# Hybrid attention encoder block on one core: order of the gate products, slots of the attention tile, loads and first bank of the merge

## Chip, core and metric

The kernel runs on one core of one Trainium2 chip, as one launch. The metric is the device time of one execution in microseconds; the three runs of the kernel before took 1425.70, 1423.99 and 1425.23 us, and the median is 1425.23 us. The execution that was profiled took 1424.24 us.

The engines are named as in the profile: PE is TensorE's matrix product and PEld its weight load, DVE is VectorE, ACT is ScalarE, POOL is GpSimd, and SP is the queue that issues almost all DMAs. SBUF is the memory that the engines compute from, PSUM the eight banks into which PE writes.

## What is computed

One encoder block on 1024 tokens of width 1024, with 16 meta tokens put in front. The part that matters here, cut from the reference:

```python
proj = h @ w_in                       # h: normed tokens; the last 2 x 1024 columns are the gates ga, gb
y_a = differential_attention(qa, ka, va, ...)     # 4 heads, two softmax maps each, 8 tiles of 128 queries
y_b = windowed_gqa(qb, kb, vb, sink)              # 8 heads, a window of 3 blocks and the meta tokens
merged = jax.nn.sigmoid(ga) * (y_a @ w_ba) + jax.nn.sigmoid(gb) * (y_b @ w_bb)
h = h + merged @ w_out
h = h + swiglu(rms_norm(h, norm_ffn), w_gate, w_up, w_down)
```

In a tile of the differential attention the first map's exponentials are combined with the second map's, each with its own sum of the row (`attn = softmax(s1) - lam * softmax(s2)`), and the combined map is multiplied with the values; the output is normed by the mean of its squares.

## The kernel before

All big products are made in a single-pass float32 form, with operands split in a high and a low half: a product of two operands is three matmuls (high x high, high x low, low x high). The parts of the program in order of time: the norm and the projections, with the windowed attention between them; the differential attention, into whose gaps the products of the gates are filled; the merge of the two branches with the gates; the output product; the feed-forward part.

**The gates.** The 2048 gate columns are eight pairs k of 128 + 128 columns (`G_COLS`). The tokens are cut in two halves, the width in two halves too, so each pair is a 2x2 block product, made with seven products p = 1 to 7 instead of eight (Strassen's scheme in Winograd's form). (k,p) is product p of pair k. It is four steps of three matmuls of 128x512, and a step is what `fill(1)` emits: one `next` of the generator `gate_steps` (line 827). `order_g` (lines 732 to 735) is the order of the 56 products. In a first phase (24 products, `first_g`) each pair has products 1, 6 and 2, then in a second phase products 5, 7, 3 and 4 of every pair. The order of pairs 0 to 3 in the first phase is made of two pairs at a time: product 1 of both, product 2 of both, so that the bank that holds (k,1) rests for a product before (k,2) adds into it. Between the two, ACT copies the bank, because the value of (k,1) alone is needed as well (line 887). Pair 4 has its products 1 and 2 one right after the other, pairs 5, 6 and 7 with product 6 among them or behind them.

**Weights of the gates.** `weights_g` (line 761) makes the operand of product n on POOL, up to three products ahead of PE (`ensure_g(n + 4)`, line 920): sums where the scheme needs them (two for product 6, lines 777 and 778), the cast to the high half (line 799) and the low half (line 800). The raw weights are loaded by `load_g` (line 747) in 512 KB pieces into four buffers, in the order in which they are used, a piece when the piece four places before it is done with. A pair k < 5 loads its first half for products 1 and 2, and both halves again for product 6 later on; a pair k >= 5 loads both halves for 1, 6 and 2.

**What is kept.** Product 6 adds to the value of product 1. For a pair k < 5 that value is stored to `u_d[k]` in HBM and read back (`k_next`, line 857) some products before its product 6; for the others it stays in SBUF (line 891). After product 6 the sum is stored to `u_d[k]` again, and read once more in the second phase, where ACT copies it into a PSUM bank (line 864) as the start of product 5.

**Token sums.** Products 6, 5, 7 and 4 need sums of token blocks, which were made earlier and lie in HBM (`t_d`). `turn_into(i)` (line 811) loads one of them (2 MB) over a block of the normed tokens `hT`: sum 2 before the first product 6 (issued behind the load `raws_g[5]`, line 818), sum 0 after (7,6), sums 1 and 3 after the last product 6 (`LAST_T`, line 808).

**Banks.** Gate products use two PSUM banks of the pool `psum2` in turn, with tags pp0 and pp1. `take` (line 849) gives a product the bank that is free and was used longest ago.

**The attention tile.** Tile n (0 to 31, four heads of eight) runs through the slots of `SLOTS` (line 41): "s" emits a piece of its scores (`scores_a`, three pieces for the second map, then three for the first; DVE reduces them at lines 980 and 984, ACT takes the exponential at 988), "t" a turn (transposition) of the tile before (`transpose_a`, ACT copies the high half at 1009, DVE subtracts the low half at 1010), "g" a gate step, and "n" a piece of the values or of the norm of tiles before that (`values_a`, line 1013, three parts for two tiles; `normed_a`, line 1023, which has a sum of squares and a factor on PE and waits between them). At the end of a tile's slots stands its combination on DVE (line 994), and the next tile's turns read its result. At the start of head 0, `G_FIRST` = 24 steps go first, at the start of the other heads `G_HEAD` = 6. Of the 224 steps `HOLD` = 22 are held back from the tiles (line 1050): they are filled in behind the last tile, one after each value part and norm piece, then the rest together.

PE's and, up to line 1100, POOL's instructions run in the order in which the program is written; the other engines' orders are chosen by the scheduler of the language, which estimates a timeline.

**Towards the merge.** As soon as the last value part frees the attention's memory (line 1127), SP loads two pieces of `w_bb` and the windowed attention's output yb (eight pieces of 256 KB, line 1142), ACT and DVE split yb (`split_yb`, line 1152; the second pair of tiles needs the memory that the gate weights leave, line 1168). The merge (line 1268) makes 32 products of 12 matmuls (`gated`, line 1256), with a sigmoid gate each. They take banks from two tags of four of the pool `psum3` in turn, "bank" (`ps_bank`) and "bank_t" (`ps_bank_t`). `psum3` takes over the banks of `psum2`; a tag gets its banks when it is first asked for.

Of the kernel before, what the change touches and what calls it, by code (L numbers as in the profile page):

```python
# [39 lines left out]
COMBINE_POOL = (0, 1, 2, 3)  # L40
SLOTS = "ssgsgntssgsgntgnt"
SLOTS_LAST = "ggggntgntnt"
S_BUFS = (2, 2)
AT_BUFS = 2
G_BUFS = 3
ROOM = 16
HOLD = 22
GT_BUFS = 4
# [26 lines left out]
def encoder_block(ctx: ExitStack, tc: tile.TileContext, x, meta, norm_mix, w_in, lq1, lk1, lq2, lk2,  # L75
                  subln, sink, w_ba, w_bb, w_o, norm_ffn, w_g, w_u, w_d, norm_final, out, dbg=None):
    nc = tc.nc
# [653 lines left out]
    G_COLS = [C_GB + 2 * k * P for k in range(4)] + [C_GA + 2 * k * P for k in range(4)]  # L731
    first_g = [(k, p) for i in (0, 2) for p in (1, 2) for k in (i, i + 1)] + [(4, 1), (4, 2)]
    first_g += [kp for k in (5, 6) for kp in ((k, 1), (k, 6), (k, 2), (k - 5, 6))]
    first_g += [(7, 1), (7, 2), (7, 6), (2, 6), (3, 6), (4, 6)]
    order_g = first_g + [(k, p) for k in range(8) for p in (5, 7, 3, 4)]
    n_first = len(first_g)

    uses_g = []
    for n, (k, p) in enumerate(order_g):
        if n >= n_first:  # L740
            uses_g.append([("s", k, 1), ("s", k, 0)] if p == 5 else [])
        else:
            uses_g.append({1: [("f", k, 0)], 2: [], 6: [("f", k, 1)] if k >= 5 else [("m", k, 0), ("m", k, 1)]}[p])
    loads_g = [u for us in uses_g for u in us]
# [16 lines left out]
    def weights_g(n):  # L761
# [3 lines left out]
        nm = f"{k}_{p}"  # L765
        kind = "s" if n >= n_first else "m" if p == 6 and k < 5 else "f"
        wa, wb = raw_g[kind, k, 0], raw_g.get((kind, k, 1))
# [3 lines left out]
        if p == 1:  # L771
            src = a11
        elif p == 2:
            src = a12
            n_freed[0] += 1 if k < 5 else 2 if k < 7 else 0
        elif p == 6:
            tt(a21, a21, a22, ALU.add)
            tt(a21, a21, a11, ALU.subtract)
            src = a21
            if k < 5 or k == 7:  # L780
                n_freed[0] += 2
        elif p == 5:
            src = sums_g[k] = gwork.tile([P, 4, P], F32, tag="s", name=f"s1g_{k}", bufs=1)
            tt(src, a21, a22, ALU.add)
        elif p == 7:
            tt(a21, a11, a21, ALU.subtract)
            src = a21
        elif p == 3:
            tt(a12, a12, a11, ALU.add)
            tt(a12, a12, sums_g.pop(k), ALU.subtract)  # L790
            src = a12
        else:
            src = a22
            n_freed[0] += 2
# [12 lines left out]
    RIGHT_G = {1: (0, 0), 6: (0, 1), 2: (1, 0), 5: (0, 0), 7: (0, 1), 3: (1, 1), 4: (1, 0)}  # L807
    LAST_T = {(7, 6): (0,), (4, 6): (1, 3)}
    INTO_T = {2: (0, 1), 0: (0, 0), 1: (0, 1), 3: (1, 0)}

    def turn_into(i):

        d, t = INTO_T[i]
        for c in (range(4) if i == 1 else (slice(0, 4),)):
            for hl, h in enumerate((hT_hi, hT_lo)):
                with ExitStack() as after:
                    if i == 2:
                        after.enter_context(tc.issue_after(raws_g[5].ins))
                    elif i == 0:
                        after.enter_context(tc.issue_after(values_in[1].ins))  # L820
                    elif i == 3:
                        after.enter_context(tc.issue_after(turned_t[0].ins))
                    to = f32(h)[:, 4 * d:4 * d + 4, HALF[t]]
                    last = nc.sync.dma_start(to[:, c], t_d[i][:, hl, c])
        turned_t[i] = last

    def gate_steps():
# [27 lines left out]
        for n, (k, p) in enumerate(order_g):  # L855
            ensure_g(n + 1)
            k_next = {(5, 1): 0, (6, 1): 1, (7, 1): 2, (7, 6): 3, (2, 6): 4, (3, 6): 0}.get((k, p), k + 1 if p == 7 and k < 7 else None)
            if k_next is not None:
# [20 lines left out]
            for c in range(4):  # L879
# [4 lines left out]
                if c == 3:  # L884
                    if p == 1:
                        p1 = kept_g(f"p1_{k}")
                        nc.scalar.copy(p1, ps)
                        if k < 5:
                            held_stores.append((u_d[k], p1))
# [194 lines left out]
    for n in range(AH * NT + T_LAG):  # L1084
# [36 lines left out]
        if n >= T_LAG and tiles[n - T_LAG][1] % 2:  # L1121
            tail.append(later(tiles[n - T_LAG]))
    n_gates[0] += HOLD
    while not valued:
        step_tail()
        fill(1)
    close_apool()
# [10 lines left out]
    for o, raw in enumerate((a11[:, 2], asum[:, 0])):  # L1138
        nc.sync.dma_start(raw.rearrange("p (c n) -> p c n", n=P), w_bb[:, o * P:(o + 1) * P].rearrange("(c p) n -> p c n", p=P))
    for j in range(4):  # L1140
        for h in range(2):
            nc.sync.dma_start((a12, w11)[h][:, j], yb_d[j // 2][j % 2 * P:j % 2 * P + P, h * 512:h * 512 + 512])
# [8 lines left out]

    def split_yb(p, j0):
        for j in (j0, j0 + 1):
            yb_t.append(p.tile([P, 2, S], F32R, name=f"yb{j}"))
        for h in range(2):
            cols = slice(h * 512, h * 512 + 512)
            for k in (j0, j0 + 1):
                split(yb_t[k][:, 0, cols], yb_t[k][:, 1, cols], (a12, w11)[h][:, k], nc.vector)

    ybpool, close_yb = pool("ybpool")  # L1160
    split_yb(ybpool, 0)
    while tail:
# [5 lines left out]
    ybpool2, close_yb2 = pool("ybpool2")  # L1168
    split_yb(ybpool2, 2)
    order_pe.__exit__(None, None, None)  # L1170
# [85 lines left out]
    def gated(i, o, half, w, src):  # L1256
# [4 lines left out]
        n_gated[0] += 1  # L1261
        ps = (ps_bank if n_gated[0] % 2 else ps_bank_t)(f"ppa_{o}_{half}_{i}")
        branch_mm(ps, w, src, tk)
# [607 lines left out]
```

## Time and profile before

| | |
|---|---|
| median of three runs | 1425.23 us |
| the profiled execution | 1424.24 us, its span 1421.9 us |
| PE busy in the span | 1401.0 us (99%) |
| DVE, ACT, POOL busy | 914.8, 672.1, 636.7 us |
| moved by DMA | 228.27 MB |
| granted TensorE clock, mean of the span | 0.998 |

All times below are in microseconds from the start of the profiled span. A row of a timeline is: start, duration, engine, line, operation, what it writes <- what it reads, sizes, count, and in brackets the idle time of the engine before it and what ended that. Matmuls overlap: a matmul of 128x512 lasts 0.39 and the next starts 0.23 after it, so a short idle time of PE in the profile is somewhat less than what was lost. A row of a list of waits is: who waited <- for whom: us in total, number, longest.

### The profile page before, as it was taken

The page shows a single profiled execution, that of the slowest core. Times are in us where ns is not written, and L with a number is a line of the kernel's source. Part 1 is how long each engine was busy: PE and PEld are TensorE (multiplying, and loading weights), DVE is VectorE, ACT ScalarE, POOL GpSimd, SP SyncE. Part 2 cuts the span into 40 slices and gives each one's busy share as a digit, 9 for nine tenths or more (in the row PEclk, how much of TensorE's full clock was granted, in tenths as well). Part 3 has the DMA queues.
Part 4 walks back from the last instruction along what each step waited for, and adds up shares of the span by engine and source line. Part 5 has one row for each costly group of instructions (what it writes and reads, how often), then busy time and mean ns, then how long its engine had stood idle before and what let it go on. Part 6 is the DMA issues. An engine that isn't in the chain of part 4 may idle for free.

```text
span 1421.9 us, 20667 instructions
## 1 busy us (share of the span) xinstructions
PE 1401.0 (99%) x7183; PEld 1202.7 (85%) x7183; DVE 914.8 (64%) x1584; ACT 672.1 (47%) x1284; POOL 636.7 (45%) x648
## 2 busy tenths in 40 slices
PE   9999999998999999999999999999999999999998
PEld 8998999987888888878888888888888888888886
DVE  6555666527787878666978956544555453787566
ACT  6355556435445555455346644333333333444454
POOL 4156865546677666322503055555545441000442
PEclk9999999999999999999999999999999999999999
DMA  8446565386896363296522724433333323954343
GB/s 235 92 128 184 154 199 160 106 290 225 259 318 211 105 209 105 68 342 198 149 103 90 207 90 148 148 106 98 101 111 104 97 97 110 353 186 144 120 128 144
DMA packets 194297, 228.27 MB, mean 161 GB/s; under 512 B 16824, under 2 KB 127360, under 8 KB 194192
## 3 DMA queue, kind: packets, MB, share of 16 engines
q1 hardware_dynamic: 192272, 224.11, 49.3%
q10 hardware_dynamic: 1920, 2.83, 0.7%
q8 instruction: 57, 0.93, 0.3%
q14 instruction: 48, 0.39, 0.1%
HBM read 152.48 MB, written 67.86 MB: 155 GB/s over the span
## 4 chain that ended last, share of the span: by engine, by line
PE 90%; DVE 4%; DMA 2%; ACT 1%; issue 1%; SPq 1%; POOL 1%; ACTq 0%; POOLq 0%; DVEq 0%
PE pg L1634 29%; PE pd L1738 14%; PE pg L881 8%; PE ppa L721 6%; PE po L1537 4%; PE pp_va L230 3%; PE pp_ka L230 3%; PE aps L977 3%; PE pp_qa L230 3%; PE apy L1019 3%; PE pp_qb L230 3%; PE bps L397 2%; PE po L1545 2%; PE bpy L437 1%; PE apt L1006 1%; PE bpt L432 1%
## 5 line engine op out<-in xcount | busy, mean ns | idle before, releaser
L1634 PE MATMUL pg<-t,wop 128*128 128x512 f32 x1056 | 242.5, 389 | 0.0
L1634 PEld LDWEIGHTS pg<-t,wop 128*128 128x128 f32 x1056 | 198.3, 188 | 41.1
L120 POOL TENSOR_TENSOR wop<-wf,wop 128x512 fp32r<-128x512 f32 x114 | 153.9, 1351 | 162.4 <-ACT wop L119 148.7
L1738 PE MATMUL pd<-ob,oa 128*128 128x512 f32 x924 | 210.1, 390 | 0.2 <-DVE ob L120 0.2
L1738 PEld LDWEIGHTS pd<-ob,oa 128*128 128x128 f32 x924 | 173.4, 188 | 36.8 <-DVE ob L120 1.0
L1634 PE MATMUL pg<-b,wop 128*128 128x512 f32 x792 | 183.3, 390 | 0.0
L1634 PEld LDWEIGHTS pg<-b,wop 128*128 128x128 f32 x792 | 148.5, 188 | 30.7
L881 PE MATMUL pg<-hT_hi,wopg 128*128 128x512 f32 x448 | 169.9, 400 | 2.7 <-POOL wopg L800 1.8
L119 ACT ACTIVATE wop<-wf 128x512 fp32r<-128x512 f32 x128 | 80.8, 633 | 73.4 <-PE pg L1634 44.3
L120 POOL TENSOR_TENSOR oa<-ra,oa 128x512 fp32r<-128x512 f32 x27 | 34.9, 1294 | 169.4 <-ACT oa L119 167.7
L119 ACT ACTIVATE oa<-ra 128x512 fp32r<-128x512 f32 x77 | 48.7, 632 | 109.0 <-PE pd L1738 50.8
L988 ACT ACTIVATE as<-as,amn 128x1040 f32<-128x1040 f32 x64 | 74.5, 1165 | 50.6 <-DVE amn L984 50.4
L881 PEld LDWEIGHTS pg<-hT_hi,wopg 128*128 128x128 f32 x448 | 84.3, 188 | 15.5 <-POOL wopg L800 2.2
L1411 DVE TENSOR_TENSOR s<-wf,wf 128x512 f32<-128x512 f32 x22 | 17.6, 798 | 112.2 <-DMA wf<-in_w_ff_up_dram 70.7
L977 PE MATMUL aps<-ak,aq 128*128 128x352 f32 (+1 forms) x384 | 86.6, 334 | 2.4 <-DVE amn L980 2.2
L881 PE MATMUL pg<-hT_lo,wopg 128*128 128x512 f32 x224 | 88.2, 394 | 0.0
L980 DVE CUSTOM_DVE_ANT_0 as<-aps,dist,far_a 128x704 f32<-128x704 f32 x64 | 60.3, 943 | 34.9 <-PE aps L977 34.6
L399 DVE CUSTOM_DVE_ANT_0 bs<-bps,tbx,nsink 128x432 f32<-128x432 f32 (+1 forms) x64 | 38.6, 629 | 61.6 <-PE bps L397 37.8
L1009 ACT ACTIVATE at<-apt 128x512 fp32r<-128x512 f32 (+1 forms) x96 | 45.4, 484 | 63.0 <-PE apt L1006 63.0
L977 PEld LDWEIGHTS aps<-ak,aq 128*128 128x128 f32 x384 | 64.2, 189 | 12.2 <-DVE amn L980 4.7
L409 POOL TENSOR_SCALAR bs<-bs,bdn 128x432 f32<-128x432 f32 (+1 forms) x64 | 36.9, 596 | 75.3 <-DVE bdn L407 34.4
L1019 PEld LDWEIGHTS apy<-at,av 128*128 128x128 f32 x400 | 54.2, 190 | 4.0
(321 smaller groups left out, 3131.1 us busy)
## 6 DMA issues: line engine op xcount, KB each, us to landing
ra<-aop SPq DMA_DIRECT2D x77, 256.0 KB, 2.7
wf<-in_w_ff_gate_dram SPq DMA_DIRECT2D x25, 512.0 KB, 3.8
wf<-in_w_ff_up_dram SPq DMA_DIRECT2D x25, 512.0 KB, 3.8
aop<-as SPq DMA_DIRECT2D x44, 256.0 KB, 2.1
w_c<-in_w_in_dram SPq DMA_DIRECT2D x17, 512.0 KB, 4.8
aop<-c SPq DMA_DIRECT2D x33, 256.0 KB, 2.0
ak<-ka_d SPq DMA_DIRECT2D x16, 520.0 KB, 6.5
t_d<-tst SPq DMA_DIRECT2D x16, 512.0 KB, 3.8
```

The lines of the kernel that those rows point to most:

```text
L119: high = nc.scalar.activation(hi, src, AF.Copy)
L120: lo_eng.tensor_tensor(lo, src, f32(hi), ALU.subtract)
L230: product = nc.tensor.matmul(ps[:, :n], a[:, c, :], b[:, c, at:at + n], start=(u == 0), stop=(u == 3 * DC - 1))
L721: nc.tensor.matmul(ps, w[:, a, j, :], src(j, b, tk), start=(j == 0 and n == 0), stop=(j == 3 and n == 2))
L881: nc.tensor.matmul(ps, op[:, x, c, :], h[:, 4 * d + c, HALF[t]], start=(p in (1, 6, 7) and c == 0 and i == 0), stop=(p in (2, 6, 3, 4) and ...
L977: nc.tensor.matmul(ps[:, :n], qs[m][:, t * P:(t + 1) * P], ks[m][:, vv, k0:k0 + n], start=(vv == 0), stop=(vv == 1))
L980: nc.vector.tensor_tensor_reduce(s[m][:, 0:2 * n].rearrange("p (a k) -> p a k", a=2), two[:, :, :n], dist[:, u0:u0 + 2 * n].rearrange("p ( ...
L988: nc.scalar.activation(s[m][:, 0:L], s[m][:, 0:L], AF.Exp, bias=mn[:, m, 1:2], scale=-1.0, accum_out=dn[:, 1:2] if m else first_sum)
L1019: nc.tensor.matmul(py[:, cols], v[:kp, a, k, :], at_[:kp, k, b, :], start=(k == 0 and j == 0), stop=(k == 8))
L1537: nc.tensor.matmul(sets_o[p][u], oa[:, a, u * P:(u + 1) * P], ob[:, b, :], start=(p in (1, 5) and j == 0 and k == 0), stop=(p in (2, 3) an ...
L1634: nc.tensor.matmul(ps, op[:, x, c, :], b[:, y, c, :], start=(p in (1, 5) and c == 0 and n == 0), stop=(p in (4, 2, 3) and c == 3 and n == ...
L1738: nc.tensor.matmul(ps[u], oa[:, a, u * P:(u + 1) * P], ob[:, b, :], start=(p in (1, 2, 5) and j == 0 and k == 0), stop=(p in (2, 3, 4) and ...
```

## The change

Six things change; no arithmetic of the result does.

- `order_g`: pairs 4 and 5 join the pattern of two pairs at a time. Then follow (6,1), (6,6), (6,2), (0,6), (7,1), (7,2), (7,6) and (1,6) to (5,6). Pair 5 now belongs to those whose product 1 goes through HBM and whose weights are loaded again for product 6, and the reads of the kept sums are put to other products.
- Token sum 2 is issued behind the load `raws_g[6]`; sums 1 and 3 follow (5,6), which is the last product 6 now.
- `SLOTS`: a gate step moves from behind the sixth score piece to ahead of the first turn. `SLOTS_LAST` has places for four gate steps, all at its front, instead of four there and a fifth behind the first turn.
- `HOLD` is 16. Behind the last tile two steps are filled in, and none between the value parts.
- yb is loaded and split by halves of the tokens: all four tiles' first half, then the second.
- `gated` begins with the other tag of banks.

```diff
-SLOTS = "ssgsgntssgsgntgnt"
-SLOTS_LAST = "ggggntgntnt"
+SLOTS = "ssgsggntssgsntgnt"
+SLOTS_LAST = "ggggntntnt"
...
-HOLD = 22
+HOLD = 16
...
-    first_g = [(k, p) for i in (0, 2) for p in (1, 2) for k in (i, i + 1)] + [(4, 1), (4, 2)]
-    first_g += [kp for k in (5, 6) for kp in ((k, 1), (k, 6), (k, 2), (k - 5, 6))]
-    first_g += [(7, 1), (7, 2), (7, 6), (2, 6), (3, 6), (4, 6)]
+    first_g = [(k, p) for i in (0, 2, 4) for p in (1, 2) for k in (i, i + 1)]
+    first_g += [(6, 1), (6, 6), (6, 2), (0, 6), (7, 1), (7, 2), (7, 6)] + [(k, 6) for k in range(1, 6)]
...
-            uses_g.append({1: [("f", k, 0)], 2: [], 6: [("f", k, 1)] if k >= 5 else [("m", k, 0), ("m", k, 1)]}[p])
+            uses_g.append({1: [("f", k, 0)], 2: [], 6: [("f", k, 1)] if k >= 6 else [("m", k, 0), ("m", k, 1)]}[p])
...
-            n_freed[0] += 1 if k < 5 else 2 if k < 7 else 0
+            n_freed[0] += 1 if k < 6 else 2 if k < 7 else 0
...
-    LAST_T = {(7, 6): (0,), (4, 6): (1, 3)}
+    LAST_T = {(7, 6): (0,), (5, 6): (1, 3)}
...
-                        after.enter_context(tc.issue_after(raws_g[5].ins))
+                        after.enter_context(tc.issue_after(raws_g[6].ins))
...
-            k_next = {(5, 1): 0, (6, 1): 1, (7, 1): 2, (7, 6): 3, (2, 6): 4, (3, 6): 0}.get((k, p), k + 1 if p == 7 and k < 7 else None)
+            k_next = {(6, 1): 0, (7, 1): 1, (7, 6): 2, (1, 6): 3, (2, 6): 4, (3, 6): 5, (4, 6): 0}.get((k, p), k + 1 if p == 7 and k < 7 else None)
...
-                        if k < 5:
+                        if k < 6:
                             held_stores.append((u_d[k], p1))
...
     n_gates[0] += HOLD
+    fill(2)
     while not valued:
         step_tail()
-        fill(1)
...
-    for j in range(4):
-        for h in range(2):
+    for h in range(2):
+        for j in range(4):
             nc.sync.dma_start((a12, w11)[h][:, j], yb_d[j // 2][j % 2 * P:j % 2 * P + P, h * 512:h * 512 + 512])
...
-    def split_yb(p, j0):
+    def open_yb(p, j0):
         for j in (j0, j0 + 1):
             yb_t.append(p.tile([P, 2, S], F32R, name=f"yb{j}"))
-        for h in range(2):
-            cols = slice(h * 512, h * 512 + 512)
-            for k in (j0, j0 + 1):
-                split(yb_t[k][:, 0, cols], yb_t[k][:, 1, cols], (a12, w11)[h][:, k], nc.vector)
+
+    def split_yb(j0, h):
+        cols = slice(h * 512, h * 512 + 512)
+        for k in (j0, j0 + 1):
+            split(yb_t[k][:, 0, cols], yb_t[k][:, 1, cols], (a12, w11)[h][:, k], nc.vector)
 
     ybpool, close_yb = pool("ybpool")
-    split_yb(ybpool, 0)
+    open_yb(ybpool, 0)
+    split_yb(0, 0)
...
-    split_yb(ybpool2, 2)
+    open_yb(ybpool2, 2)
+    for j0, h in ((2, 0), (0, 1), (2, 1)):
+        split_yb(j0, h)
...
-        ps = (ps_bank if n_gated[0] % 2 else ps_bank_t)(f"ppa_{o}_{half}_{i}")
+        ps = (ps_bank_t if n_gated[0] % 2 else ps_bank)(f"ppa_{o}_{half}_{i}")
```

More of the change, by code (lines that the diff above doesn't have):

```diff
@@ L765, in weights_g @@
         nm = f"{k}_{p}"
-        kind = "s" if n >= n_first else "m" if p == 6 and k < 5 else "f"
+        kind = "s" if n >= n_first else "m" if p == 6 and k < 6 else "f"
         wa, wb = raw_g[kind, k, 0], raw_g.get((kind, k, 1))
@@ L779, in weights_g @@
             src = a21
-            if k < 5 or k == 7:
+            if k < 6 or k == 7:
                 n_freed[0] += 2
```

## The prediction

> **What bounds the kernel now.** I read the page first, then the busy time by stretches of 50 us, then the list of waits of the whole execution, and last the timelines around each wait.
>
> ```profile
> span 1421.9 us, 20667 instructions
> PE 1401.0 (99%) x7183; PEld 1202.7 (85%) x7183; DVE 914.8 (64%) x1584; ACT 672.1 (47%) x1284; POOL 636.7 (45%) x648
> ...
> 290.00:615.00 325.00, 314.21 (x1868) 277.69 (x1866) 228.69 (x508) 160.38 (x296) 199.91 (x232) 1.00 0.61 204
> ...
> 400.00:450.00 50.00, 48.77 (x299) 43.29 (x298) 41.58 (x93) 25.87 (x48) 39.69 (x44) 1.00 0.84 295
> ...
> 600.00:650.00 50.00, 49.15 (x222) 40.12 (x221) 29.74 (x42) 28.18 (x48) 14.80 (x12) 1.00 0.94 312
> 650.00:700.00 50.00, 50.00 (x222) 41.26 (x221) 42.27 (x53) 20.15 (x35) 20.34 (x14) 1.00 0.51 157
> ```
>
> The columns after the stretch are its length and the busy us of PE, weight load, DVE, ACT and POOL. TensorE is the bound: 1401.0 of 1421.9 us. The whole change lies between 290 and 615 us (differential attention with the gate products filled in) and in the merge behind it. There TensorE idles 325.00 - 314.21 = 10.8 us, and behind it nothing is left to win: 650 to 700 us is full. The change adds and removes no matrix product, so 10.8 us bounds the gain, and the question is which waits end. Here they are:
>
> ```profile
> PE apt L1006 <- DVE at L1010: 2.3, 4, 0.8
> PE aps L977 <- DVE amn L980: 2.2, 7, 0.4
> PE pg L881 <- POOL wopg L800: 1.8, 1, 1.8
> PE apt L1006 <- DVE as L994: 1.7, 1, 1.7
> ...
> PE apt L1006 <- DVE adn L991: 1.0, 1, 1.0
> ...
> PE pg L881 <- ACT p L887: 0.8, 1, 0.8
> PE ppa L721 <- DVE g L912: 0.8, 1, 0.8
> ...
> PEld aps L977 <- DVE amn L980: 4.7, 10, 0.6
> ```
>
> Total, number and longest stand behind each pair; the last row is of the stretch 290 to 660. The seven PE rows add to 10.6 us. Each one that stands once is one place, and four of those five are places that the change rewrites.
>
> **The change, part by part.** I write (k,p) for product p of gate pair k, a step for a quarter of it (three matmuls), and count steps in the program's order to find the tile in which each falls.
>
> The price of a step, and the four places:
>
> ```profile
> 376.18 4.12 PE pg L881 x18
> ...
> 324.61 0.53 PE L881 MATMUL pg<-hT_hi,wopg 128*128 128x512 f32 x1 [0.85 <-ACT p L887]
> ...
> 338.89 0.51 PE L881 MATMUL pg<-hT_hi,wopg 128*128 128x512 f32 x1 [1.76 <-POOL wopg L800]
> ...
> 592.29 0.66 PE L1006 MATMUL apt<-ident,as 128*128 128x128 f32 x4 [1.72 <-DVE as L994]
> ...
> 615.11 7.11 PE L721 MATMUL ppa<-yb,wbhb 128*128 128x512 f32 x30 [0.78 <-DVE g L912]
> ```
>
> Eighteen matmuls are six steps, so one step is 4.12/6 = 0.69 us.
>
> *a. Pairs 4 and 5 in one another's gaps.* At 324.61 (4,2) waits 0.85 us, because it adds into the bank of (4,1), which ACT must copy first. After, (5,1) stands between them in the other bank. But its weights are barely there:
>
> ```profile
> 322.74 1.29 POOL L800 TENSOR_TENSOR wopg<-wg_f,wopg 128x512 fp32r<-128x512 f32 x1
> ...
> 328.82 1.29 POOL L777 TENSOR_TENSOR wg_f<-wg_f 128x512 f32<-128x512 f32 x1 [4.80 <-DMA wg_f<-in_w_in_dram]
> ...
> 313.87 0.36 SPq L824 DMA_DIRECT2D hT_hi<-t_d  x1
> 316.56 0.36 SPq L824 DMA_DIRECT2D hT_lo<-t_d  x1
> ...
> 319.33 0.39 SPq L757 DMA_DIRECT2D wg_f<-in_w_in_dram  x1
> ```
>
> The low half of (5,1), tenth or eleventh on POOL, ended at 322.74 + 1.29 = 324.03, when TensorE was free at 323.76. A gain between 0 (POOL keeps that order and is late) and 0.85; I take 0.55, as two thirds of the wait is nearer to these rows than none.
>
> *b. The product that waited for a load.* At 338.89 TensorE waits 1.76 us for the weights of (5,6), whose load was issued at 319.33 behind the 2 MB of the token sum (the two hT rows) and landed 9.5 us later, at 328.82. After, this place computes (5,2) from a load that POOL already had at 322.74, (6,6) comes two products later, and the token sum (two DMAs of 1 MB) is issued behind one more weight load. It is not needed before (6,6) either, so it has as much time as before. So the wait goes. Does it come back at the next stop? The chain behind a tile's turn starts from TensorE's own scores and shifts along with them, so I take 1.76, with 0.8 as the low end (the wait of 1.0 on L991, two turns later, grows to twice its length).
>
> *c. A new wait.* (7,1) and (7,2) are products 16 and 17 now. Steps 66 to 71 are the six filled in one go at the head of attention head 1: the last two of (7,1), then all of (7,2), in one bank. In place of (7,1) stands (6,2) now, and its copy shows the price:
>
> ```profile
> 377.17 0.63 PE L881 MATMUL pg<-hT_hi,wopg 128*128 128x512 f32 x2
> ...
> 377.61 0.59 ACT L894 COPY g<-pg 128x512 f32<-128x512 f32 x1 [1.11 <-PE pg L881]
> ```
>
> The first matmul of the row at 377.17 ends (6,2) at 377.56, the second begins the next product some 0.24 after it, at 377.41. ACT is free (1.11 us idle), starts 0.05 after the end and is done at 378.20, so TensorE would go on at about 378.25: a loss of 0.8, for all that is queued behind on it, the next tile's scores first. Low end 0.6; high end 2.0, if an exponential of 1.17 us goes ahead on ACT (the row in d).
>
> *d. The moved gate steps.* A tile keeps six score pieces, five gate steps and three turns; one gate step goes from behind the sixth score piece to ahead of the first turn. Between a tile's last scores and the turn that needs its combination there are four gate steps before and after, so the cover of that chain does not grow. What changes is that the second turn comes one step (0.69 us) sooner, so its eviction (L1010) can be over before the combination (L994) starts:
>
> ```profile
> 365.24 1.16 ACT L988 ACTIVATE as<-as,amn 128x1040 f32<-128x1040 f32 x1
> ...
> 325.06 1.28 DVE L994 SCALAR_TENSOR_TENSOR as<-as,adn,as 128x1040 f32<-128x1040 f32 x1
> ...
> 366.85 2.25 DVE L994 SCALAR_TENSOR_TENSOR as<-as,adn,as 128x1040 f32<-128x1040 f32 x1
> 369.02 0.87 DVE L1010 TENSOR_TENSOR at<-apt,at 128x512 fp32r<-128x512 f32 x2
> 369.82 0.93 DVE L980 CUSTOM_DVE_ANT_0 as<-aps,dist,far_a 128x704 f32<-128x704 f32 x1
> ...
> 366.70 1.30 POOL L800 TENSOR_TENSOR wopg<-wg_m,wopg 128x512 fp32r<-128x512 f32 x1
> ```
>
> Now the order on DVE is combination, two evictions (0.87), then the reduction that the next scores wait for. Taking the evictions out of that row could give up to 3.0, two thirds of the 4.5 us that the waits on L1010 and on L980 hold. Other way: if the second turn's copy on ACT now goes ahead of the exponential, the chain is longer by some 0.5 us where the scores are already waiting, ten places by the PEld row: a loss of 5. I take a gain of 0.5, near nothing, because the chain and its cover stay.
> A rule speaks against even that. The combination took 2.25 us beside a POOL weight step (366.70) and 1.28 alone. The Trainium skill (SBUF — State Buffer, Who interferes with whom) says that a VectorE instruction with two SBUF inputs contends with a GpSimd instruction that reads SBUF; the trace agrees, with 0.97 us in this row. By it the eviction order would not matter in the tiles that meet a POOL step, and the sum would be 3.2, without this 0.5.
>
> *e. The last tile.* At 592.29 the last combination is waited for, 1.72 us, because the gate budget is spent. After (16 steps held back instead of 22, shorter last slots) one gate step and four more stand in that place.
>
> ```profile
> 586.97 0.47 PE L977 MATMUL aps<-ak,aq 128*128 128x336 f32 x2
> ...
> 597.88 0.99 PE L1019 MATMUL apy<-at,av 128*128 128x256 f32 x7
> ```
>
> The chain took from the last scores to the turn 592.29 - 586.97 = 5.3 us. The cover will be five steps (3.45) and two value parts (0.99 and more each), 5.4, with the factor's and the second turn's transpositions on top. The wait goes: 1.72, between 1.0 and 2.1 (with 0.4 of a wait on L980 one turn earlier).
>
> *f. The merge.* Of the steps behind the last value part (ended 598.87) 14 stay of 20. Now that stretch lasts to 615.11 - 0.78 = 614.33, 15.5 us: 20 steps of 0.69 and 1.7 of other work. After: 14 x 0.69 + 1.7 = 11.3. Its first product waits 0.78 for L912, the eviction of (7,4). As each pool's banks lie in the order in which they are first asked for, asking the other tag first gives the first product the same bank again, but the new product order puts (7,3) there, which ACT copies. What that copy stands behind:
>
> ```profile
> 611.40 1.68 ACT L119 ACTIVATE yb<-m 128x512 fp32r<-128x512 f32 x3 [2.31 <-DMA m<-yb_d]
> 613.09 1.28 ACT L1260 ACT_TABLE_LOAD   x1
> 614.38 0.63 ACT L1260 ACTIVATE gt<-gt 128x512 f32<-128x512 f32 x1
> 614.92 0.57 ACT L910 COPY g<-pg 128x512 f32<-128x512 f32 x1
> ```
>
> Behind splits that wait for loads, a table load and a sigmoid: 615.49, 16.6 us after the value parts' end at 598.87. If that order stays, the merge (every product of it stands behind the first) waits 16.6 - 11.3 = 5.3, a loss of 4.5; if the copy goes ahead of the splits, 0.78 is won. (7,3) is finished 4.1 us sooner against the loads, so I expect it among the splits, a wait of about 0.8: no gain. Loading yb by halves makes the four first pieces land first, so the product itself need not wait.
>
> *Hidden.* Pair 5's weights are loaded once more and its first product goes through memory: 512 KB and twice 256 KB, on queues that move 228 MB; its store and reload lie several products apart. The token sum behind (7,6) (2 MB) is issued two products sooner on SP, the reloads of the kept sums start two products later and end at the same one. These cost nothing as long as POOL has weights ahead (second rival).
>
> Sum: 0.55 + 1.76 - 0.8 + 0.5 + 1.72 + 0 = 3.7 us. The profiled execution took 1424.24 (2.3 outside its span), so 1420.5; it stands 1.0 below the median of 1425.23, which puts the median after at 1421.5.
>
> **The rivals.**
>
> *1. Given back at the merge.* The copy of (7,3) goes behind the last split: that ended at 611.40 + 1.68 = 613.08, 14.2 after the value parts; with 0.57 for the copy and 11.3 to the merge the wait is 3.5, 2.7 more than now: 1424.2, no change. For it: the order now. Against: (7,3) is ready sooner. If the table load stood ahead too, its row adds 1.28.
> The Trainium skill (ScalarE: Activation LUTs, What ACT_TABLE_LOAD costs) gives such a load 1283 ns and a drain of 1380 ns behind it. The row has the 1.28, and the sigmoid starts at its end, so the drain is not seen here; with it this wait would be 1.4 longer.
>
> *2. Five sixth products in a row (slower).* (1,6) to (5,6) now follow one another, each needing 1 MB of loads and four POOL steps, and a load waits until the weights of two products earlier are made. Place: tiles 8 to 12. Price: 1.76 each, as seen at 338.89, four times = 7.0, so 1428.5. It decides when POOL ends a low half after its product's first step. For it:
>
> ```profile
> 401.32 1.31 POOL L800 TENSOR_TENSOR wopg<-wg_m,wopg 128x512 fp32r<-128x512 f32 x1
> ...
> 406.60 0.39 PE L881 MATMUL pg<-hT_hi,wopg 128*128 128x512 f32 x1
> ```
>
> (3,6), second of three in a row now, is ready only 406.60 - 402.63 = 4.0 us ahead. Against: POOL is busy 39.69 of 50 us in that stretch, its work in all is the same, and the run starts with pair 7's products made early.
>
> *3. The exponential comes later* (d's bad end): 1421.5 + 0.5 + 5 = 1427.0.
>
> **How the numbers follow.** Forecast 0.55 (its own range 1418.5 to 1422.4), rival 1 0.25, rival 3 0.05, rival 2 0.15. A measurement here tells about 0.2%, 2.9 us, from no change: faster 0.55, same 0.30 (rivals 1 and 3), slower 0.15. The range reaches from 1417.5 (d at 3.0, f at 0.78, a and e at their high ends) to 1428.0, which leaves out most of rival 2 and little below.
>
> **What would show it.** No wait of pg on POOL near 337, none on ACT near 324, a new one of 0.7 to 0.8 on ACT in the six steps at about 375; no wait on L994 in the last tile; at the merge the first ppa waiting for ACT's copy (L910's line) and not for DVE. Idle time between 290 and 612 should be near 7 us. I am wrong if pg waits for POOL between 385 and 415, if the aps waits grow beyond ten, or if ppa waits over 2 us.

## The result and the profile after

The changed kernel is slower: median 1430.53 us over eight runs (1428.18 to 1435.58) against 1424.93 for the kernel before in the same sitting, a ratio of 1.0047 with the 95% interval 1.0031 to 1.0064. The prediction was 1421.5 in a range up to 1428.0. The profiled execution is the slowest of the eight, 1435.58 us, so its places are read rather than its total.

From the page and the busy time by stretches of the kernel after (columns as in the prediction; the last three numbers are the mean granted TensorE clock, the DMA share and GB/s):

```profile
span 1433.8 us, 20684 instructions
...
295.80:627.40 331.60, 314.29 (x1843) 277.23 (x1842) 224.61 (x504) 158.67 (x294) 202.70 (x232) 0.99 0.60 201
```

This stretch reaches from the first gate product to the merge's start. Before, the same work ran from 293.5 to 615.1, 321.6 us with 310.7 of them busy. So it takes 10.0 us more: TensorE idles 17.3 us where it idled 10.9, and its busy time grew by 3.6 us, at a granted clock of 0.99 instead of 1.00. Behind the merge's start the two executions take the same time (806.4 and 806.8 us), and 2.3 us of the difference between them lie ahead of the stretch, in a part that the change leaves as it is. So the loss lies where the change lies. The list of waits of the kernel after follows (who <- for whom: total, number, longest). Its lines are those of the changed file: 880 there is 881 before, and so for all lines quoted here between 735 and 1120. Where a kernel further down has lines added, its turns, combination and evictions stand up to four lines further on; the names of the tiles tell which is which.

```profile
PE apt L1005 <- DVE at L1009: 7.6, 14, 1.0
PE apt L1005 <- DVE adn L990: 3.1, 3, 1.8
PE pg L880 <- POOL wg_s L789: 2.4, 1, 2.4
PE apt L1005 <- POOL as L994: 2.0, 1, 2.0
...
PE aps L976 <- DVE amn L979: 0.7, 2, 0.4
PE apst L1031 <- ACT ysq L1025: 0.7, 1, 0.7
PE pg L880 <- ACT p L886: 0.7, 1, 0.7
```

Three of the forecast's readings came true: no product waits for the weights of a sixth product any more, the last tile no longer waits for its combination, and the new wait of 0.7 us on ACT's copy of (7,1) is there. But the turns' waits on the evictions of the turns before them (L1009) went from 2.3 us in 4 places to 7.6 us in 14, the waits put down to `adn` (L990) went from 1.0 us in one place to 3.1 in three, and there are two single waits of 2.0 and 2.4 us that were not there. None of the prediction's three signs of being wrong came (POOL between 385 and 415, more than ten waits of the scores, over 2 us at the merge's first product): nothing in it watched the evictions.

### The profile page after: what moved, and what is told of

Its sections match the earlier page's. It is cut to its first block, busy times and chain, and to the rows that moved or that the text cites. A ratio compares the mean times of both kernels' runs of the same rounds, so it can differ in the third digit from the quotient of the medians.

```text
span 1433.8 us, 20684 instructions
## 1 busy us (share of the span) xinstructions
PE 1404.6 (98%) x7183; PEld 1205.8 (84%) x7183; DVE 915.6 (64%) x1584; ACT 671.1 (47%) x1284; POOL 636.6 (44%) x648
## 4 chain that ended last, share of the span: by engine, by line
PE 89%; DVE 4%; DMA 3%; issue 2%; SPq 1%; ACT 1%; POOL 0%; ACTq 0%; DVEq 0%; POOLq 0%
PE pg L1637 29%; PE pd L1741 14%; PE pg L880 7%; PE ppa L721 6%; PE po L1540 4%; PE aps L976 3%; PE pp_ka L230 3%; PE pp_va L230 3%; PE pp_qa L230 3%; PE apy L1018 3%; PE apt L1005 2%; PE pp_qb L230 2%; PE bps L397 2%; PE po L1548 2%; PE bpy L437 1%
## 5 line engine op out<-in xcount | busy, mean ns | idle before, releaser
L880 PE MATMUL pg<-hT_hi,wopg 128*128 128x512 f32 x448 | 166.8, 404 | 3.1 <-POOL wg_s L789 2.4
L1005 PE MATMUL apt<-ident,as 128*128 128x128 f32 x288 | 47.8, 276 | 12.9 <-DVE at L1009 7.6
```

Source lines behind the costliest of these rows:

```text
L880: nc.tensor.matmul(ps, op[:, x, c, :], h[:, 4 * d + c, HALF[t]], start=(p in (1, 6, 7) and c == 0 and i == 0), stop=(p in (2, 6, 3, 4) and ...
L1005: nc.tensor.transpose(pt[:kp, j, :], s[:, k * P:k * P + kp], ident)
```

## The experiments

Each was timed in five rounds beside the kernel before. Its median there lay between 1424.02 and 1424.72 us.

| kernel | median us | ratio to before, 95% interval |
|---|---|---|
| slots_alone | 1429.89 | 1.0040 (1.0027 to 1.0052) |
| after_old_slots | 1425.75 | 1.0010 (1.0001 to 1.0019) |
| order_alone | 1429.23 | 1.0029 (1.0019 to 1.0039) |
| tail_alone | 1422.92 | 0.9991 (0.9982 to 1.0000) |
| slots_comb_first | 1428.87 | 1.0029 (1.0018 to 1.0041) |
| slots_scores_later | 1435.04 | 1.0074 (1.0059 to 1.0089) |
| slots_evict_first | 1424.31 | 1.0002 (0.9993 to 1.0011) |
| slots_turn_back | 1429.88 | 1.0041 (1.0028 to 1.0053) |
| after_comb_first | 1430.13 | 1.0035 (1.0022 to 1.0048) |
| turn3_last | 1422.32 | 0.9985 (0.9974 to 0.9995) |
| after_turn3_last | 1427.02 | 1.0020 (1.0011 to 1.0029) |
| turn3_comb_first | 1423.30 | 0.9996 (0.9987 to 1.0005) |
| after_both_repairs | 1425.88 | 1.0013 (1.0004 to 1.0022) |
| order_turn3_last | 1424.22 | 1.0001 (0.9992 to 1.0009) |

### Which part loses

Four kernels: SLOTS alone; the change without its SLOTS; the pair order (with `LAST_T`, `k_next`, `raws_g[6]` and the bounds k < 6) alone; the rest (`SLOTS_LAST`, `HOLD`, yb by halves, first bank) alone.

```diff
 slots_alone, against the kernel before
-SLOTS = "ssgsgntssgsgntgnt"
+SLOTS = "ssgsggntssgsntgnt"
 after_old_slots, against the kernel after
-SLOTS = "ssgsggntssgsntgnt"
+SLOTS = "ssgsgntssgsgntgnt"
```

> The kernel before with the changed order within a tile (SLOTS) and nothing else. Theory SLOTS (the second turn now stands right behind the sixth score piece, so first and second turns wait on DVE's evictions): the loss is here, 1429 to 1432 us, 1.003 to 1.005 of before, with turn waits on L1009's evictions at 10 or more places (2.3 us at 4 places before). Theory ORDER (the new pair order asks for loads sooner than the queues bring them): 1424 to 1426 us, 0.999 to 1.001.

> The changed kernel with the old order within a tile; pair order, late loads, last tile and merge stay as changed. Theory SLOTS: the loss goes and the small gains stay, 1421 to 1424 us, 0.997 to 0.999, at most 5 turn waits on evictions. Theory ORDER: the loss stays, 1428 to 1431 us, with the wait on the reload of u_0 near 428 and that on the gate weights' load near 334 still there.

> The kernel before with the pair order, the second sum's later read and the later turn load alone (old SLOTS, old last tile, old merge). Theory SLOTS: 1423 to 1426 us, 0.999 to 1.001. Theory ORDER: 1428 to 1431 us, 1.002 to 1.005, with one wait near 334 and one near 428 of about 2 us each.

> The kernel before with the last tile's order, the number of steps held back, the halves of the merge's splits and the merge's first bank alone. Both theories: 1422 to 1424.5 us, 0.998 to 1.000, without the 1.7 us wait of the last tile's turn. A third theory, that the steps taken from the end are missed there: 1426 us or more.

Neither theory held alone: each of the two changes loses by itself. SLOTS costs 1429.89 - 1424.59 = 5.3 us by itself, and the pair order 4.6 us by itself, though with a spread of 1426.05 to 1431.88; the rest wins 1.7 (interval 0 to 2.6). After_old_slots came out 1.75 us above the top of what theory SLOTS gave it. So there are two losses to explain.

### The loss of SLOTS: what DVE does first

The gate step that stood behind the sixth score piece now stands ahead of the first turn, and so ahead of the last three score pieces. So from a tile's last score piece to the next tile's first two pieces there is now one gate step instead of two. DVE timelines around one tile's combination, first in the kernel before, then in slots_alone, there with the row of the first turn on PE:

```profile
439.20 0.27 DVE L993 TENSOR_SCALAR adn<-asum,adn,neglam 128x1 f32<-128x1 f32 x1 [0.73 <-ACT as L988]
439.51 1.30 DVE L994 SCALAR_TENSOR_TENSOR as<-as,adn,as 128x1040 f32<-128x1040 f32 x1
440.73 0.87 DVE L1010 TENSOR_TENSOR at<-apt,at 128x512 fp32r<-128x512 f32 x2
441.53 0.93 DVE L980 CUSTOM_DVE_ANT_0 as<-aps,dist,far_a 128x704 f32<-128x704 f32 x1
```

```profile
442.52 0.27 DVE L993 TENSOR_SCALAR adn<-asum,adn,neglam 128x1 f32<-128x1 f32 x1 [1.25 <-ACT as L988]
442.98 0.95 DVE L980 CUSTOM_DVE_ANT_0 as<-aps,dist,far_a 128x704 f32<-128x704 f32 x1 [0.19 <-PE aps L977]
443.86 0.08 DVE L980 DVE_READ_ACCUMULATOR2_ANT amn<- 128x1 f32 x1
443.86 1.49 DVE L994 SCALAR_TENSOR_TENSOR as<-as,adn,as 128x1040 f32<-128x1040 f32 x1
445.27 0.87 DVE L1010 TENSOR_TENSOR at<-apt,at 128x512 fp32r<-128x512 f32 x2
...
446.10 0.63 PE L1006 MATMUL apt<-ident,as 128*128 128x128 f32 x4 [0.77 <-DVE at L1010]
```

Before, the combination starts 0.04 us after the factor (L993 ends at 439.47), the two evictions follow, and the next tile's reduction (L980) is last. In slots_alone the reduction stands between factor and combination; combination and evictions end 1.2 us later, counted from the factor (446.14 - 442.52 = 3.6 against 441.60 - 439.20 = 2.4), and the first turn, which takes a bank that these evictions free, waits 0.77. DVE runs in the order that the scheduler of the language chose, and that order changed although no DVE instruction was touched: in slots_alone DVE sits idle 0.19 us for the scores of the reduction, although the factor of the combination is done at 442.79. Four kernels pin or shift that order:

```diff
 slots_comb_first: slots_alone, and around the reduction of L980
+                    with ExitStack() as after:
+                        if m and comb_a:
+                            after.enter_context(tc.issue_after(comb_a[-1].ins))
 slots_evict_first: slots_alone, and there
+                            for op in comb_a[-1:] + lo_a[-1:]:
+                                after.enter_context(tc.issue_after(op.ins))
 slots_scores_later, against the kernel before
-SLOTS = "ssgsgntssgsgntgnt"
+SLOTS = "ssgsgntgssgsntgnt"
 slots_turn_back, against slots_alone
-SLOTS = "ssgsggntssgsntgnt"
+SLOTS = "ssgsggntssgsgntnt"
```

Here `comb_a` lists the combinations (L994) and `lo_a` the evictions (L1010) in the order of the program, and `issue_after` queues the reduction behind them on DVE. The expectations give the lines as in the kernel after, one less.

> The kernel before with the changed SLOTS, and the next tile's first reduction (L979) queued on DVE behind this tile's combination (L993). Theory DVE ORDER (with the scores a gate step later, the next tile's first reduction is ready before the combination's factor and DVE takes it first, 0.93 us, so that combination and the evictions behind it come about 1 us late and the first turn of every second tile waits): the loss of slots_alone (1429.9 us) goes, 1422 to 1426 us, waits of turns on L1009's evictions at most 3 us in total instead of 8.9. Rival CLOSENESS (the second turn simply stands too near the scores and its own bank): 1428 us or more, still 7 us or more of such waits.

> The kernel before with only the last three score pieces a gate step later in the tile; the first turn stays where it was. Theory DVE ORDER: the late combination is there as in slots_alone and the first turn now comes a gate step (0.69 us) sooner after it, so the waits on evictions are larger than in slots_alone: 1432 to 1445 us, more than 12 us of waits. Rival CLOSENESS OF THE FIRST TURN (what costs is that the first turn was moved): 1424 to 1427 us.

> The kernel before with the changed SLOTS; on DVE the next tile's first reduction is queued behind this tile's combination and behind the evictions of the turns before it. With the combination alone in front, 428.9 us and 6.5 us of waits on evictions were left, the first turns' 0.42 us each behind the 0.93 us reduction. Theory TWO WAITS (the first turn's wait is DVE order, the second turn's 0.3 us in every norm tile is its closeness to the first turn, whose bank it takes): the first turns' waits from tile 6 on go, about 3 us of second turns' waits stay, 1426 to 1428 us. Rival (all is closeness): no change, 1428 to 1430 us.

> The kernel before with the changed SLOTS, but the gate step between the second and the third turn put back in front of the second. Theory TWO WAITS: the second turn's 0.3 us waits (3.1 us in slots_alone) go and the first turn's stay, since scores and first turn stand where they stood: 1426 to 1428.5 us. Rival (all the loss is DVE order): 1429 to 1431 us, as slots_alone.

Putting the combination alone in front gave back 1.0 us only, a miss for the theory as first put: the reduction then stood between combination and evictions, and 6.5 us of waits on evictions stayed. With the evictions in front as well the whole loss of 5.3 us went (1424.31, level with before), more than either theory had expected. The list of waits of slots_alone, then of slots_evict_first, and the timeline of the same tile in slots_evict_first, DVE and the first turn on PE:

```profile
PE apt L1006 <- DVE at L1010: 8.9, 15, 1.7
PE apt L1006 <- DVE as L994: 2.1, 2, 1.3
```

```profile
PE apt L1010 <- DVE as L998: 2.3, 2, 2.1
...
PE apt L1010 <- DVE at L1014: 1.5, 2, 1.0
```

```profile
438.96 1.30 DVE L998 SCALAR_TENSOR_TENSOR as<-as,adn,as 128x1040 f32<-128x1040 f32 x1
440.18 0.87 DVE L1014 TENSOR_TENSOR at<-apt,at 128x512 fp32r<-128x512 f32 x2
440.98 0.93 DVE L984 CUSTOM_DVE_ANT_0 as<-aps,dist,far_a 128x704 f32<-128x704 f32 x1
...
441.28 0.60 PE L1010 MATMUL apt<-ident,as 128*128 128x128 f32 x4
```

The old order is back with the new SLOTS, and the turn at 441.28 waits for nothing. The rival that the second turn stands too close falls with this kernel: the second turn stands there as in slots_alone, and the loss is gone. Slots_turn_back, which gives the second turn its gate step back and takes it from the third, won nothing (1429.88), against theory TWO WAITS. Moving only the scores later costs more, as forecast: 1435.04, with the first turn a step nearer to the late evictions; the waits on evictions rose less than forecast, to 9.8 us, and 6.8 us more were put down to combination and factor. The times also show that the changed SLOTS by itself wins nothing once the order is repaired: 1424.31 against 1424.02. The kernel before with the order edge and the old SLOTS was not run, so it stays open whether the edge wins something by itself.

### The loss of the pair order: one more load in a queue that is full

Near 425, product (0,5) waits in every profile of the new pair order with the old place of token sum 3, between 1.2 and 3.3 us. Timelines of SP (the issues), POOL, ACT and PE; first the kernel before, then after, then after_old_slots:

```profile
411.81 0.35 SPq L860 DMA_DIRECT2D u<-u_d  x1
420.18 0.59 ACT L864 COPY pg<-u 128x512 f32<-128x512 f32 x1
```

```profile
408.84 0.43 SPq L823 DMA_DIRECT2D hT_hi<-t_d  x1
409.32 0.97 SPq L823 DMA_DIRECT2D hT_lo<-t_d  x1
410.40 2.39 SPq L756 DMA_DIRECT2D wg_s<-in_w_in_dram  x1
...
418.84 2.76 SPq L859 DMA_DIRECT2D u<-u_d  x1
...
419.76 1.30 POOL L799 TENSOR_TENSOR wopg<-s1g,wopg 128x512 fp32r<-128x512 f32 x1
...
427.24 0.59 ACT L863 COPY pg<-u 128x512 f32<-128x512 f32 x1
...
427.93 0.47 PE L880 MATMUL pg<-hT_hi,wopg 128*128 128x512 f32 x1 [2.40 <-POOL wg_s L789]
```

```profile
424.80 0.59 ACT L863 COPY pg<-u 128x512 f32<-128x512 f32 x1 [1.96 <-DMA u<-u_d]
...
425.49 0.77 PE L880 MATMUL pg<-hT_hi,wopg 128*128 128x512 f32 x1 [3.28 <-POOL wopg L798]
```

The profile names POOL, but the operand of (0,5) was made by 419.76 + 1.30 = 421.06, and the product starts 0.10 us after ACT's copy of the kept sum u_0 into its bank (427.24 + 0.59), in after_old_slots as well (424.80 + 0.59). The copy needs the reload of u_0: in the kernel after this lands 8.4 us behind its issue, at 427.24, just when the copy starts, and in after_old_slots ACT sits idle 1.96 us for it. The reload is issued at 418.84 instead of 411.81, 6.7 us before TensorE is free for the product (427.93 - 2.40) instead of 10.0 (421.77 - 411.81). SP's queue holds, ahead of it, token sum 3 (the two hT rows at 408.84, 2 MB), loads of the second phase's weights and a store, and the issues take up to 4.7 us each there, where 0.4 is common. In the kernel before token sum 3 stands ahead of the reload too (404.06), but two weight loads of the second phase are issued ahead of it; with the one load more of the new order only one is, and the next comes between token sum 3 and the reload (410.40). Nothing reads token sum 3 before the first product 4, which follows (0,5) by some 20 us. So it was put behind token sum 1 (the expectations call it the fourth turn's load):

```diff
 turn3_last: after_old_slots, and
                     elif i == 3:
-                        after.enter_context(tc.issue_after(turned_t[0].ins))
+                        after.enter_context(tc.issue_after(turned_t[1].ins))
```

> The changed kernel with the old SLOTS (1425.75 us so far) and the load of the fourth turn of the hidden half (2 MB, read only by product 4) issued behind that of the second instead of in front of the gate weights' load. Theory QUEUE (the new pair order has one weight load more, which now lies behind 4 MB of turn loads on SP, lands at 420 instead of 405, and makes POOL's weights and PE wait 1.2 to 3.3 us near 425): that wait goes, 1421 to 1424 us, with a smaller spread. Rival (the loss of the order is the earlier waits up to 340): 1425 to 1427 us.

> The changed kernel whole, new SLOTS included, with the fourth turn's load issued behind the second's. If the two losses (SLOTS, and the weights' load behind the turn loads) stand side by side, the 3.4 us that this gave with the old SLOTS come again: 1426 to 1428 us against 1430.5, no wait of 2 us near 425. If the loss of SLOTS covers it: 1429 to 1431 us.

> The kernel before with the pair order alone and the fourth turn's load issued behind the second's: what the pair order is worth without the late weights. By the forecast's terms a, b and c: 1.5 us faster than before, 1423 us. Theory HANDED ON (the waits taken away at 324 and 339 come back in part as the first turn's of tiles 1 and 2, 1.6 and 0.5 us): 1423.5 to 1425 us. If the pair order loses by itself: 1426 us or more.

Turn3_last runs at 1422.32, 3.4 us less than without that line, and faster than the kernel before and the kernel after. On the whole change the same line wins 3.5 (1430.53 to 1427.02), and on the pair order alone 5.0 (1429.23 to 1424.22). Each of these pairs was timed in two sittings; counted from the kernel before beside it, the gains are 3.6, 2.6 and 4.8. The smaller spread that was expected did not come (1419.15 to 1427.66). The line was not tried on the kernel before. The same place in turn3_last:

```profile
415.63 0.37 SPq L859 DMA_DIRECT2D u<-u_d  x1
...
419.94 0.59 ACT L863 COPY pg<-u 128x512 f32<-128x512 f32 x1 [4.90 <-DMA u<-u_d]
```

Against after_old_slots, from which this line alone divides it, the reload is issued 3.7 us sooner (415.63 instead of 419.30) and lands 4.3 instead of 5.5 us behind its issue. The copy is done at 420.53, ahead of its product at 421.96. The queue was the cause, as theory QUEUE had it, but the late piece on the path was the kept sum's reload and not the weights that the expectation named.

### What the pair order is worth without that

Order_turn3_last is level with the kernel before: 1.0001, where the terms a, b and c asked for 1.5 us and theory HANDED ON for 1423.5 to 1425 (1424.22). DVE and PE around the first turn of tile 1, in the kernel before and then in turn3_last:

```profile
324.67 0.27 DVE L993 TENSOR_SCALAR adn<-asum,adn,neglam 128x1 f32<-128x1 f32 x1
324.86 0.27 DVE L1010 TENSOR_TENSOR at<-apt,at 16x128 fp32r<-16x128 f32 x1
...
326.49 0.63 PE L1006 MATMUL apt<-ident,as 128*128 128x128 f32 x4
```

```profile
324.38 0.27 DVE L992 TENSOR_SCALAR adn<-asum,adn,neglam 128x1 f32<-128x1 f32 x1
324.63 0.57 DVE L983 CUSTOM_DVE_ANT_0 as<-aps,far_m,amn 128x336 f32<-128x336 f32 x1
...
325.33 1.28 DVE L993 SCALAR_TENSOR_TENSOR as<-as,adn,as 128x1040 f32<-128x1040 f32 x1
...
326.75 0.63 PE L1005 MATMUL apt<-ident,as 128*128 128x128 f32 x4 [1.59 <-DVE adn L990]
```

Before, the wait of 0.85 us that ends at 324.61 kept TensorE back, so that it came to this turn at 326.49, behind the combination's end (325.06 + 1.28, the row in part d of the prediction); the turn waits for nothing. Without that wait TensorE is there at 326.75 - 1.59 = 325.16, a reduction (L983, 0.57) goes ahead of the combination, and the turn waits 1.59 us. It starts 0.26 us later than before: the gain of step a went to that turn.

> The changed kernel with the old SLOTS, the fourth turn's load behind the second's, and the next tile's first-map reductions queued behind the combination on DVE. Theory HANDED ON (taking the 0.85 us wait of (4,2) away let the next tile's reduction overtake the combination, so that the first turn of tile 1 now waits 1.59 us): that wait falls to 0.5 us or less, 1420 to 1421.8 us against 1422.3. Rival (the combination is late by the exponential, not by order): 1422 to 1423.5 us.

> The changed kernel whole, with the next tile's first reduction queued behind the combination on DVE. Theory DVE ORDER: 1424 to 1427 us against 1430.5 of the changed kernel. Rival CLOSENESS: 1429 to 1432 us.

> The changed kernel whole, new SLOTS included, with both repairs: the next tile's first reduction queued on DVE behind combination and evictions (1429.9 to 1424.3 us on SLOTS alone), and the fourth turn's load issued behind the second's (1430.5 to 1427.0 us on the changed kernel). If these two causes are the whole loss, what is left are the forecast's other terms (a, b, c, e, f: 3.2 us of gain, 1.5 to 2.5 us of it seen so far): 1420 to 1423 us, faster than before. If something else is lost with all parts together: 1424 us or more.

Turn3_comb_first cut the 1.59 us wait to 0.62, a little more than the 0.5 expected, so the order made most of that wait. It won no time (1423.30 against 1422.32, intervals that overlap): a wait of 2.40 us came at the next tile's third turn. POOL and PE there:

```profile
330.13 1.26 POOL L776 TENSOR_TENSOR wg_f<-wg_f 128x512 f32<-128x512 f32 x1 [5.65 <-DMA wg_f<-in_w_in_dram]
331.33 1.25 POOL L997 COPY as<-as 128x32 f32<-128x32 f32 x1
...
332.64 0.33 PE L1008 MATMUL apt<-ident,as 128*128 128x128 f32 x1 [2.40 <-POOL as L997]
```

POOL's small copy for the turn is queued behind a gate weight's step that waits 5.65 us for its load. The kernel after has the same pair of rows (a wait of 6.11 us on the load, the turn 2.04 us late). The load is that of (6,6), the first product 6: the late load of part b still holds TensorE there, by way of POOL's order.

After_comb_first and after_both_repairs are the kernel after with the order edge of slots_comb_first, and with that of slots_evict_first and the line of turn3_last; turn3_comb_first is turn3_last with the edge of slots_comb_first. After_comb_first came to 1430.13, as the rival had it: like slots_comb_first it leaves the reduction ahead of the evictions. After_both_repairs missed its range: 1425.88, 4.65 us better than the kernel after but 1.5 slower than before (1424.39). Its list of waits:

```profile
PE apt L1009 <- DVE at L1013: 3.0, 4, 1.0
PE aps L976 <- DVE amn L983: 2.0, 6, 0.4
PE pg L880 <- POOL wopg L799: 1.5, 2, 1.2
PE apt L1009 <- POOL as L998: 1.4, 1, 1.4
```

The evictions' waits fell from 7.6 to 3.0 us (before 2.3) and the scores wait as they did before (2.0, before 2.2), but POOL is late twice and holds a turn once, 2.9 us together (before 1.8). So the two causes are the larger part of the loss and not all of it. What else is lost with all parts together is not shown: the new SLOTS and the pair order together at POOL were not tried apart.

## Why the prediction was wrong

- **d, the moved gate steps**, is the step that failed most: forecast +0.5 "because the chain and its cover stay", measured -5.3 (slots_alone). The chain was counted in gate steps, and that count was right. What was not counted is what else becomes ready on DVE inside the chain: with one step less between a tile's last scores and the next tile's first, the next reduction is ready before the combination and goes ahead of it and of the evictions. Rival 3 had the size, 5 us, and gave it a chance of 0.05, but by another mechanism (the exponential behind a copy on ACT). The tile of slots_alone above does not have it: ACT is idle for 1.69 us before the exponential at 441.23 and waits for DVE. The row with the order "combination, two evictions, then the reduction" was in the prediction; that this order is the scheduler's choice, and may turn, was not asked.
- **The part called hidden** is the second: "These cost nothing as long as POOL has weights ahead" was forecast 0 and measured about -3.5 (after against after_turn3_last; -2.6 counted from the kernel before of each sitting). The count of products between issue and use was the same before and after, but not what stands ahead in SP's queue: one more weight load, and 2 MB of token sum 3 ahead of the loads that are needed sooner.
- **a and b**: both waits went as said, 0.85 and 1.76, but in turn3_last the tiles' chain hands most of it back, 1.59 and 0.51 at the first turns of tiles 1 and 2 and 0.31 at a third turn; a, b and c together came to 0.2 us instead of 1.5 (order_turn3_last). That the chain behind a tile's turn "shifts along" with the scores failed: it starts from the scores, which the wait stood behind, and so the wait had been its cover. In the kernel after b's late load holds TensorE in another way: (6,6), which comes two products later, does not wait for its weights, but POOL waits 6.11 us for the load, and the turn whose copy stands behind that on POOL waits 2.04; what else POOL holds was not asked. **c**: 0.7, forecast 0.8.
- **e** was right: the 1.72 us wait is gone, and tail_alone, which holds e and f, wins 1.7 us (interval 0 to 2.6). **f** was right in its sum, by luck and not by its parts: the wait on ACT's copy at the merge's first product, forecast as 0.8, did not come in the kernel after, and a wait of 0.7 for the norm's squares (L1025), which was not forecast, stands in its place.
- **Rival 1** did not come. **Rival 2** (five sixth products in a row) had the nearest time, 1428.5, and did not come in kind: between 385 and 415 no product waits for POOL's weights.
- The terms as measured, 5.3 + 3.5 lost and 0.2 + 1.7 won, make 6.9 of loss (6.0 with the 2.6 of above); the kernel after lost 5.6. The difference is within the intervals, so whether the terms add is not shown.

## What to carry to other kernels

When an instruction moves on one engine, write down which instructions become ready earlier or later on the other engines and whether a scheduler may reorder them; a chain's cover counted on the moved engine alone is no bound, and an order edge (one line) keeps the sequence that the timing relies on. A transfer's price is set by what stands ahead of it in its queue, so a load that nobody needs for 20 us goes behind the one that is needed next. A short wait that is removed is often the cover of the next one: ask what is late after it before it is booked as won.

## What the runs showed of the hardware

A wait of some 2 us can cost more than itself. Stretches of 5 us in the kernel after, around its waits of 2.04 (at 334.79) and 2.40 us (at 427.93):

```profile
330.00:335.00 5.00, 2.96 (x18) 2.33 (x17) 2.74 (x6) 3.03 (x5) 1.68 (x3) 1.00 1.09 371
335.00:340.00 5.00, 5.00 (x20) 4.25 (x20) 3.28 (x8) 1.84 (x4) 5.00 (x5) 0.66 0.58 183
...
425.00:430.00 5.00, 2.60 (x12) 2.06 (x11) 3.47 (x7) 2.54 (x5) 5.00 (x5) 0.84 1.08 365
430.00:435.00 5.00, 5.00 (x27) 4.45 (x27) 1.70 (x5) 1.73 (x3) 5.00 (x7) 0.82 1.01 375
```

The granted clock falls to 0.66, and to 0.84 and 0.82; from 428.50 to 431.17 the matmuls of 128x512 last 0.63 us instead of 0.39. The work lost by it is about 1.7 us each time, an estimate from these clocks (5 x 0.34, and 5 x 0.16 + 5 x 0.18). In turn3_last every 5 us stretch from 415 to 435 has 1.00. A wait of 2.1 us does not always do it: at 339 slots_alone shows 0.89 and 0.77 in the two stretches from 335 to 345, and tail_alone 1.00 in both. The wide spread of some kernels with such waits (order_alone 1426 to 1432) may come from this; no run shows it, and the five times of slots_alone lie within 0.9 us. The Trainium skill (TensorE: Matmul & The Clock Gate, Part 1: The HAM clock gate) lets the clock fall after an idle window of about 3.4 us that runs freely; the dependence on the moment agrees, but the waits here are shorter than that window, and the measurement decides.
